# Full-row score products, grouped SSM output products, and new planner prices in a two-block fp32 kernel

## The chip, the cores and the metric

The kernel runs on one core of a Trainium2 chip. The metric is the time of one execution on the device, in microseconds (us). The engines are TensorE (PE: matmuls and transposes; PEld: its weight loads), VectorE (DVE), ScalarE (ACT), GpSimd (POOL) and SyncE (SP, which issues DMAs). Each runs its own instructions in order, and they wait for one another through semaphores.

## What is computed

The reference is two transformer blocks, one after the other, on 512 tokens of 1024 channels, in float32. The first has NSA attention (compressed, selected and windowed keys; at this length the last two reach the same 512 keys), MLA attention and an MLP with squared ReLU; its norms are modulated by `c @ w_ada`. The second has a diagonal state-space mixer (SSM) beside an eight-head attention with a relative bias, then a gated FFN.

```python
# block 1
mod = c @ w_ada + b_ada
h = modulate(rmsnorm(x, g_mix), sh_a, sc_a)
z = h @ w_in
s = einsum('bghqd,bgkd->bghqk', qq, k_win) * scale - slopes * dist
...
y = sigmoid(zga) * (o_nsa @ w_o_nsa) + sigmoid(zgb) * (o_mla @ w_o_mla)
x = x + gt_a * (y @ w_out)
x = x + gt_m * (square(relu(h @ w_fc1)) @ w_fc2)
# block 2
_, states = associative_scan(combine, (a, bu), axis=1)
y = einsum('bsgp,ghp->bsgh', states, c_mat).real + d_skip * uf
...
x = x + mixed @ w_out
x = x + (silu(h2 @ w_gate) * (h2 @ w_up)) @ w_down
```

## The kernel before

**Precision.** A float32 product is done in three passes. A value is split into a rounded high part and a low part (`hilo`, names ending in h and l), and `mm` adds h*h, l*h and h*l in PSUM. Weights arrive as `wr`, become `wh` on ScalarE and `wl` on VectorE, or on POOL for some stages. So the dense layers are rows such as `mm<-hh,wh`, `mm<-hl,wh`, `mm<-hh,wl` of 512 columns.

**How work is ordered.** The kernel's functions do not issue instructions. `Rec` hands each to `Plan.record`, which notes what it reads and writes; `Plan.price` (line 121) gives it a time; `Plan.schedule` (line 159) then plays a list schedule: each engine takes, at its planned free time, the ready instruction of the lowest number, within a window of 500, provided its tiles find a place. An instruction with a second engine (`alt`) goes there if the first would end later. `Plan.issue` emits all in that order; its call stands on line 337, so every row of the profile reads L337 and is told apart by its tiles. The planner's prices decide nothing but this order: on the chip an engine runs its instructions in order and each waits for its semaphores.

**Attention.** `Unit` (line 1256) is one head, or one of two halves of an NSA head (16 units in NSA, 8 in MLA, 8 in the second attention). `qk(i)` writes the scores of query block i into a bank `S` of 128 to 512 columns, by the products that `passes(i)` lists; VectorE adds the bias (`sb`, `st`), ScalarE takes the exponential, `sc` scales, `tr` transposes on PE into a bank `T` (`T<-ident,sb`), `ph` and `pl` are made from it, `pv` multiplies by the values into `O`. `pipeline` (line 1321) staggers three units; dense jobs run between.

A query tile `qA` holds the high part on 64 of the rows and the low part on the other 64. `kA` holds the keys' high part on both halves, so the first product, of 128 rows, gives q_hi*k_hi + q_lo*k_hi. The second takes the 64 rows of q_hi with `kL`, the keys' low part. In NSA `kL` has the low part on both halves. In the second attention `k2l` is one tile for two heads, each on its half.

**SSM.** `ssm(hf)` (line 1905) does half of the channels. X products (`T<-U,rec`, 64 columns wide, 64 of them) turn inputs `U`, read back from DRAM (`ud`), into chunk inputs; VectorE rotates them (`sr`, `si`) and does a scan per pair (`tensor_tensor_scan`); the products by the rotation (`ss`, `st`, on VectorE or POOL) give the states; then the Y products: for each of o and e one bank Y, and for each of four k one product of `U` with 128 rows and two of the states with `pcr` and `pci`, of 64 rows each (rows `T<-U,rec 128*128` and `T<-ss,rec 64*128`), after which ScalarE copies Y.

**The start.** For each of eight tiles of 128 channels, VectorE and POOL sum 1024 rows of `w_ada` weighted by `c` into `aacc` and `aacg` (the weights `aw` come by SP's queue), PE adds these over partitions (`S<-ones,aacc`), VectorE makes the scale `ca`, then scales the tile (`xT`) and splits it (`hh` on ScalarE, `hl` on VectorE). `linT4` multiplies each tile with four weight pieces into four banks as it comes.

Of the kernel before, what the change touches and what calls it, by code (L numbers as in the profile page):

```python
# [19 lines left out]
T = 512  # L20
# [17 lines left out]
BGP = 300  # L38
ORDER = {"N": "Q3 Q2 S3 V0 T0 Q1 S2 V123 F T1 Q0 S1 S0 T23",
# [4 lines left out]
class Op:  # L44
    __slots__ = ("eng", "fn", "a", "kw", "prio", "tiles", "cost", "nbytes", "succ", "npred", "ready", "idx", "alt")


class Plan:
    """Records the instructions of the engines, with what they read and write, and issues them in the order of a
    list schedule: each engine takes the instruction of the lowest number of those whose operands are there."""  # L50
# [24 lines left out]
    def record(self, eng, name, fn, a, kw, alt=None):  # L75
# [39 lines left out]
        o.cost = self.price(o, name, out[0], aps)  # L115
        if alt is not None:
            o.eng = alt
            o.alt = (alt, getattr(self.eng[alt], name), self.price(o, name, out[0], aps))
            o.eng = eng

    def price(self, o, name, out, aps):
        """An estimate of the instruction's time, in us."""
        ins = [x for x in aps if x is not out]
        n = max([x.free_size() if callable(x.free_size) else x.free_size for x in aps]) if aps else 1
        ps = any(x.space == PSUM for x in aps)
        if name == "dma_start":
            sz = 4
            for d in out.shape:
                sz *= d
            o.nbytes = sz  # L130
            return 1.0 if o.eng == "POOL" else 0.06
        if o.eng == "PE":
            l, r = o.a[1], o.a[2]
            if name == "transpose":
                return 0.107 * (out.shape[-1] if len(out.shape) == 2 else 128) / 128
            cols = 1
            for d in r.shape[1:]:
                cols *= d
            if r.dtype == F32R:
                return max(cols, 16) / 2400.0  # L140
            return max(cols * 4 / 2400.0, 0.21 if l.shape[-1] > 64 else 0.107)
        if o.eng == "ACT":
            c = n / 1200.0 + (0.052 if ps else 0.093)
            if name == "activation" and (hasattr(o.kw.get("scale"), "tensor") or hasattr(o.kw.get("bias"), "tensor")):
                c += 0.093
            if o.kw.get("accum_out") is not None:
                c += 0.093
            return c
        if o.eng == "DVE":
            if name in ("tensor_scalar", "tensor_copy") and not ps:  # L150
                return 0.069 + n / 1920.0
            if name == "memset":
                return 0.01 + n / 960.0
            return 0.069 + n / 960.0
        if name == "memset":
            return 0.04 + n / 1200.0
        return 0.12 + n / 250.0 if name == "tensor_scalar" else 0.95 if n <= 8 else 0.15 + n / 475.0

    def schedule(self, window):
        """Operations in the order of their planned starts. A place for a tile is given ahead of its turn only if  # L160
        what comes before that turn can still be run, one by one, in the places that are left."""
# [30 lines left out]
        hw = dma = 0.0  # L192

# [11 lines left out]
        def lacking(i):  # L205
            """The tag of which the operation can't have a place now."""
# [15 lines left out]
        while len(order) < n:  # L222
# [21 lines left out]
            if o.alt is not None and e == o.alt[0]:  # L244
                # the second engine takes it if the first one would end later
# [4 lines left out]
                cost, fn = o.alt[2], o.alt[1]  # L250
            g = lacking(i)
# [17 lines left out]
            end = s + cost  # L269
            free[e] = end  # L270
            if o.nbytes:
# [6 lines left out]
                dma = d + o.nbytes / 360e3  # L278
# [61 lines left out]
class Rec:  # L340
    """An engine whose instructions are recorded; alt is a second engine that may take them."""
# [9 lines left out]
class Later:  # L351
    """Instructions that are to come some steps later in their engine's order."""
# [21 lines left out]
class Weights:  # L374
# [24 lines left out]
    def split_next(self, limit):  # L399
        """Split the next piece into its two parts, if the slots are free."""  # L400
# [36 lines left out]
def merge(gens):  # L437
    """Emit several streams side by side; gens is a list of (generator, total cost)."""
# [18 lines left out]
def offset(plan, g, d):  # L457
    """The stream with its numbers shifted by d."""
# [23 lines left out]
def tile_kernel(ctx: ExitStack, tc: tile.TileContext, A, out):  # L482
# [29 lines left out]
    def early(name):  # L512
        """A tile that may be written long before its turn: these share a few places of their own."""
# [19 lines left out]
    def prio(d):  # L533
        """Instructions that are to come as if traced d instructions later."""
# [5 lines left out]
    # ---------------------------------------------------------------- constants  # L540
# [50 lines left out]
    def rstd_of(acc, n, tag="T"):  # L591
        """[tokens] rsqrt of the mean of squares, along the partitions: [128, 4]."""
# [8 lines left out]
    def spread(r, tag="T"):  # L601
        """[128 tokens, 4] -> the same row of 512 tokens on each partition (in PSUM)."""
# [11 lines left out]
    # ---------------------------------------------------------------- dense jobs  # L614
# [7 lines left out]
    def linT(srcs, kk, nk, xs, evac, mt=2, tag="mm", first=None):  # L622
        """out^T tiles: srcs are pieces [128, kk*(mt*128)]; xs() gives the (hi, lo) list."""
# [21 lines left out]
    def linT4(srcs, kk, nk, xs, evacs, tags=("mm", "mm", "O", "S"), pre=None, vec=None):  # L645
        """Two jobs side by side, k outermost: for inputs that come one after the other."""
# [27 lines left out]
    def linV(srcs, kk, nk, xs, evac, n=256, tag="mm"):  # L674
        """out tiles [128 tokens, n]: x as the stationary operand."""
# [29 lines left out]
    def run(upto):  # L705
        """Emit the jobs up to (not including) number upto."""
# [50 lines left out]
    # ---------------------------------------------------------------- block 1, inputs of the attentions  # L757
# [88 lines left out]
    def q_parts(p, e, scale):  # L846
        """[hi; lo] (or [lo; hi]) of one head of the pair of heads in p; hi stays on its partitions."""
# [83 lines left out]
    # MLA projections  # L931
# [61 lines left out]
    # outputs of the attentions  # L993
# [50 lines left out]
    # MLP  # L1044
# [43 lines left out]
    # block 2  # L1088
# [16 lines left out]
    def qk2_evac(j):  # L1105
        def ev(m, p):
# [118 lines left out]
    def last_gen():  # L1225
        """The last rows of w_down: tokens on the partitions, so that they can leave tile by tile."""
# [125 lines left out]
    def o_fin(key, h, store, cb):  # L1352
        """o of head h = upper + lower half; both heads of a pair go into one tile."""
# [16 lines left out]
    # ---------------------------------------------------------------- start  # L1370
# [12 lines left out]
    def ada0_vec(j):  # L1383
        """Shift and scale of the channels 128 j ..: the products, summed over the tiles of rows."""
# [66 lines left out]
    def go(gen, every=5.0):  # L1451
        """Emit a stream; every so often a step of the background."""
# [19 lines left out]
    # ---------------------------------------------------------------- NSA  # L1472
# [54 lines left out]
    def nsa_units():  # L1527
# [11 lines left out]
        for h in range(8):  # L1539
            g = h // 4  # L1540
            r = 64 * (h % 2)
            for b in range(2):
                def passes(i, b=b, g=g, h=h, r=r):
# [4 lines left out]
                    return [(qA[:, cs], kA[:, :n]), (qA[r:r + 64, cs], kL[r:r + 64, :n])]  # L1548
# [641 lines left out]
```

## Time and profile before

| what | value |
|---|---|
| time, median of 3 runs | 1551.39 us (1551.03 to 1553.93) |
| span of the profiled execution | 1547.8 us |
| mean granted TensorE clock in it | 0.970 of full speed |
| PE busy | 1473.4 us, 95%, 7008 instructions |
| PEld busy | 1193.4 us, 77% |
| DVE busy | 994.4 us, 64%, 1972 instructions |
| ACT busy | 627.0 us, 41% |
| POOL busy | 273.6 us, 18%, 262 instructions |

Busy shares are averages over stages that differ. In time they are: the start (0 to 67 us), projections and the compression MLP (to 138), NSA (to 340), MLA and its outputs (to 468), the MLP (to 940), the SSM's first half (to 997), the second attention with the SSM's second half (to 1116), the mixer's output (to 1180), the FFN (to 1548). A PE row shows a modelled end, and rows overlap; how far apart starts are tells what a product takes.

### The profile page before, as it was taken

The numbers are of one execution on the slowest core, as the hardware profiler recorded it, in microseconds if no ns is written. First come the engines' busy times: TensorE is split into PE (matmuls) and PEld (weight loads), VectorE is DVE, ScalarE is ACT, GpSimd is POOL, SyncE is SP. The second block draws the span as 40 slices with busy tenths as digits, with TensorE's granted clock in tenths as the row PEclk, the third lists the DMA queues.
The fourth block names the chain that finished last, engine by engine and source line by source line (L and its number), as shares of the span: only waits on it lengthen the run. The fifth ranks groups of instructions, "written<-read, shape, count | busy, mean of one in ns | idle before, by whom it ended". The sixth has DMA issues, their size and how long they took to land.

```text
span 1547.8 us, 19040 instructions
## 1 busy us (share of the span) xinstructions
PE 1473.4 (95%) x7008; PEld 1193.4 (77%) x7008; DVE 994.4 (64%) x1972; ACT 627.0 (41%) x1057; POOL 273.6 (18%) x262
## 2 busy tenths in 40 slices
PE   4889999998899999999999998999899999999997
PEld 3687777786688888887787887877688888888885
DVE  7835687877997788766443556296876544553544
ACT  3425556665654342332323431274733322231222
POOL 7514040535200000000213111037031000000000
PEclk9998999999999999999999998699899999999998
DMA  9355252434026422333444665113122333333311
GB/s 368 110 181 173 68 168 84 137 109 170 28 94 202 128 76 89 109 105 126 132 146 160 218 225 109 41 56 116 51 93 82 97 108 90 101 95 110 104 60 55
DMA packets 72604, 184.75 MB, mean 119 GB/s; under 512 B 16792, under 2 KB 17640, under 8 KB 72512
## 3 DMA queue, kind: packets, MB, share of 16 engines
q1 hardware_dynamic: 63424, 158.62, 32.2%
q0 software_dynamic: 7552, 22.97, 4.4%
q10 hardware_dynamic: 1536, 1.95, 0.4%
q8 instruction: 55, 0.90, 0.2%
q14 instruction: 37, 0.30, 0.1%
HBM read 165.41 MB, written 19.67 MB: 120 GB/s over the span
## 4 chain that ended last, share of the span: by engine, by line
PE 78%; DVE 9%; issue 5%; DMA 4%; POOL 2%; ACT 2%; SPq 0%; DVEq 0%; POOLq 0%; ACTq 0%
PE mm L337 64%; PE T L337 7%; PE S L337 4%; PE O L337 3%; DVE sb L337 2%; DMA aw<-in_w_ada 2%; POOL aacg L337 1%; DMA adaw<-in_w_ada 1%; DVE wl L337 1%; DVE pl L337 1%; DVE zqd L337 1%; DMA U<-ud 1%; DVE q L337 1%; DVE sr L337 1%; DVE xt L337 0%
## 5 line engine op out<-in xcount | busy, mean ns | idle before, releaser
L337 PE MATMUL mm<-hh,wh 128*128 128x512 f32 x880 | 363.4, 415 | 13.3 <-ACT hh L337 5.8
L337 ACT CAST wh<-wr 128x1024 fp32r<-128x1024 f32 x209 | 219.2, 1051 | 366.1 <-PE mm L337 331.0
L337 PE MATMUL mm<-hl,wh 128*128 128x512 f32 x880 | 355.1, 403 | 0.2 <-DVE hl L337 0.2
L337 PE MATMUL mm<-hh,wl 128*128 128x512 f32 x880 | 352.8, 401 | 0.5 <-DVE wl L337 0.5
L337 DVE TENSOR_TENSOR wl<-wr,wh 128x1024 fp32r<-128x1024 f32 x199 | 256.3, 1289 | 144.8 <-ACT wh L337 142.3
L337 PEld LDWEIGHTS mm<-hh,wh 128*128 128x128 f32 x880 | 167.9, 192 | 52.6 <-ACT hh L337 6.6
L337 PEld LDWEIGHTS mm<-hh,wl 128*128 128x128 f32 x880 | 168.8, 192 | 37.7 <-issue 1.4
L337 PEld LDWEIGHTS mm<-hl,wh 128*128 128x128 f32 x880 | 169.2, 192 | 34.7 <-issue 2.4
L337 PE MATMUL mm<-fh,wl 128*128 128x512 f32 x416 | 162.5, 391 | 0.0
L337 PE MATMUL mm<-fl,wh 128*128 128x512 f32 x416 | 162.3, 390 | 0.0
L337 PE MATMUL mm<-fh,wh 128*128 128x512 f32 x416 | 161.7, 390 | 0.0
L337 PEld LDWEIGHTS mm<-fh,wh 128*128 128x128 f32 x416 | 78.1, 188 | 16.8 <-issue 0.6
L337 PEld LDWEIGHTS mm<-fh,wl 128*128 128x128 f32 x416 | 78.1, 188 | 16.8 <-issue 0.6
L337 PEld LDWEIGHTS mm<-fl,wh 128*128 128x128 f32 x416 | 78.1, 188 | 16.6 <-DVE PBr L337 0.2
L337 ACT ACTIVATE sb<-sb,st 128x256 f32<-128x256 f32 (+3 forms) x128 | 71.5, 560 | 47.4 <-DVE st L337 46.5
L337 POOL TENSOR_TENSOR adacc<-adacc,adaw 128x1024 f32<-128x1024 f32 x28 | 68.9, 2460 | 55.1 <-ACT adaw L337 54.6
L337 PE MATMUL T<-ident,sb 128*128 128x128 f32 x320 | 57.7, 280 | 11.1 <-DVE sb L337 6.0
L337 DVE TENSOR_TENSOR pl<-T,ph 128x384 fp32r<-128x384 f32 (+1 forms) x96 | 56.9, 595 | 16.5 <-ACT ph L337 13.6
L337 ACT CAST ph<-T 128x384 fp32r<-128x384 f32 (+1 forms) x96 | 49.0, 511 | 44.9 <-PE T L337 35.6
L337 POOL TENSOR_TENSOR st<-st,mhalf 128x1 f32<-128x1 f32 x4 | 2.2, 547 | 358.2 <-DVE st L337 358.2
L337 PEld LDWEIGHTS T<-ident,sb 128*128 128x128 f32 x320 | 40.3, 143 | 22.8 <-DVE pl L337 6.2
L337 DVE CUSTOM_DVE_ANT_0 sb<-S,nb 128x256 f32<-128x256 f32 (+2 forms) x96 | 45.3, 482 | 15.6 <-PE S L337 15.0
(373 smaller groups left out, 2560.4 us busy)
## 6 DMA issues: line engine op xcount, KB each, us to landing
wr<-in_w_fc SPq DMA_DIRECT2D x64, 512.0 KB, 3.6
wr<-in_w_in SPq DMA_DIRECT2D x48, 512.0 KB, 4.4
wr<-in_w_gu SPq DMA_DIRECT2D x44, 512.0 KB, 3.6
adaw<-in_w_ada POOLq DMA_DIRECT2D x32, 512.0 KB, 4.3
wr<-in_w_down SPq DMA_DIRECT2D x22, 512.0 KB, 3.5
aw<-in_w_ada SPq DMA_DIRECT2D x32, 256.0 KB, 6.0
wr<-in_w_out SPq DMA_DIRECT2D x16, 512.0 KB, 3.8
rec<-srec SPq DMA_DIRECT2D x28, 256.0 KB, 5.8
```

The source lines that it names most:

```text
L337: fn(*o.a, **o.kw)
```

## The change

Three things are changed; docstrings and comments go as well, which moves the issuing call from line 337 to 359.

First, the second score product takes all 128 rows, in NSA and in the second attention. It then adds q_lo*k_lo in NSA. In the second attention there is a `k2l` tile for each head, whose other half POOL sets to zero: eight memsets of 64x512 more.

Second, the Y products of the SSM: both banks of an o are open, the eight `U` products stand first, then for each k the four 64-row products of both e.

Third, the planner: other prices; a charge `SWITCH` of 0.2 us when a PE instruction has another count of rows or columns (32, 64 or 128) than the one before it; and a lock `port` between VectorE and POOL, held by VectorE's instructions with two inputs in SBUF, or one in a copy or tensor_scalar, and by all of POOL's but memsets and DMAs.

```diff
+SWITCH = 0.2
...
-            return 1.0 if o.eng == "POOL" else 0.06
+            return 0.6 if o.eng == "POOL" else 0.06
         if o.eng == "PE":
             l, r = o.a[1], o.a[2]
+            m, cut = free(l), lambda v: 32 if v <= 32 else 64 if v <= 64 else 128
+            o.mode = (cut(l.ap[0][1]), 128 if name == "transpose" or r.dtype == F32R else cut(m))
...
-                return max(cols, 16) / 2400.0
+                return max(0.11, free(r) / 2400.0 + 0.0136)
...
+            o.port = len(big) > 1 or (two and len(big) == 1)
...
+        o.port = True
+        if name == "tensor_copy":
+            return 0.06 + n / 1040.0
+        return 0.1 + n / 355.0 if name == "tensor_scalar" else 0.95 if n <= 8 else 0.15 + n / 475.0
...
+            if o.port and port[other[e]] > s:
+                heapq.heappush(f, (port[other[e]], r, i))
+                continue
...
             end = s + cost
+            if e == "PE":
+                end += SWITCH * (o.mode != mode)
+                mode = o.mode
+            if o.port:
+                port[e] = end
...
-                kl = slot(F32R, "k2l")
                 for e in range(2):
-                    kA = slot(F32R, "k2A")
+                    kA, kl = slot(F32R, "k2A"), slot(F32R, "k2l")
                     r, o = e * 64, (1 - e) * 64
+                    gp.memset(f(kl)[o:o + 64], 0.0)
...
-                    return [(qA[:, cs], kA[:, :n]), (qA[r:r + 64, cs], kL[r:r + 64, :n])]
+                    return [(qA[:, cs], kA[:, :n]), (qA[:, cs], kL[:, :n])]
...
+            Y = [bank("T")[:, 0:256].rearrange("p (g c) -> p g c", g=4) for e in range(2)]
             for e in range(2):
...
+                    mm(Y[e][:, k], rec[2 * o + g // 4][:, 128 * (g % 4):128 * (g % 4) + 128], U[:, 8 * o + g], k == 0,
+                       False)
+                yield 0.9
+            for k in range(4):
+                for w, (pc, s_) in enumerate(((pcr, sr), (pci, si))):
+                    for e in range(2):
+                        r = slice(64 * e, 64 * e + 64)
+                        mm(Y[e][:, k], pc[r, 128 * k:128 * k + 128], s_[r, k], False, w == 1)
```

The rows below are the instructions in the order in which they are issued; the number behind a name tells tiles of one name apart.

On PE, at the Y products of the SSM's first half (`rec` 1859 and 1860 are the full-row matrices, 1867 and 1869 are `pcr` and `pci`), before:

```order
L337 MATMUL mm_1896<-hh_1796,wl_1876 128x512
L337 MATMUL T_1898<-ss_1883,rec_1867 128x64
L337 MATMUL mm_1896<-hh_1804,wh_1886 128x512
L337 MATMUL T_1898<-ss_1883,rec_1869 128x64
L337 MATMUL T_1898<-U_1873,rec_1859 128x64
L337 MATMUL T_1898<-ss_1883,rec_1867 128x64
L337 MATMUL T_1898<-ss_1883,rec_1869 128x64
L337 MATMUL T_1898<-U_1873,rec_1860 128x64
```

and with the change:

```order
L359 MATMUL T_1899<-U_1873,rec_1859 128x64 x2
L359 MATMUL T_1899<-U_1873,rec_1860 128x64 x2
L359 MATMUL mm_1896<-hh_1788,wh_1875 128x512
L359 MATMUL mm_1896<-hl_1789,wh_1875 128x512
L359 MATMUL mm_1896<-hh_1788,wl_1876 128x512
L359 MATMUL T_1898<-ss_1883,rec_1867 128x64
L359 MATMUL T_1899<-ss_1883,rec_1867 128x64
L359 MATMUL T_1898<-ss_1883,rec_1869 128x64
L359 MATMUL T_1899<-ss_1883,rec_1869 128x64
```

The `U` products now stand together ahead of the first `ss`, and the 64-row products come by fours of both banks.

On POOL, at the same place, where VectorE does its scans, before:

```order
L337 MEMSET ss_1992 128x512
L337 TENSOR_TENSOR wl_1900<-wr_1851,wh_1899 128x1024
L337 TENSOR_TENSOR wl_1910<-wr_1854,wh_1909 128x1024
L337 TENSOR_TENSOR ss_1894<-sr_1892,rec_1872 128x4x63
L337 TENSOR_TENSOR st_1893<-sr_1892,rec_1872 128x4x63
```

and with the change:

```order
L359 TENSOR_TENSOR ss_1883<-sr_1881,rec_1871 128x4x63
L359 TENSOR_TENSOR st_1882<-sr_1881,rec_1871 128x4x63 x2
L359 TENSOR_TENSOR wl_1910<-wr_1854,wh_1909 128x1024
L359 MEMSET ss_2064 128x512
```

One of the two `wl` has left POOL, and the other stands behind products for the first `ss`.

On VectorE at the start, where the second tile is scaled (`S_182` carries its sums), before:

```order
L337 TENSOR_SCALAR aacc_207<-aw_142,vec 128x256
L337 SCALAR_TENSOR_TENSOR aacc_192<-aw_140,vec,aacc_192 128x256
L337 SCALAR_TENSOR_TENSOR aacc_207<-aw_142,vec,aacc_207 128x256
L337 SCALAR_TENSOR_TENSOR ca<-S_182,ca,vec 128x1
L337 SCALAR_TENSOR_TENSOR aacc_207<-aw_143,vec,aacc_207 128x256
L337 SCALAR_TENSOR_TENSOR xT_117<-xT_117,ca,R_162 128x512
```

and with the change:

```order
L359 SCALAR_TENSOR_TENSOR aacc_217<-aw_189,vec,aacc_217 128x256
L359 SCALAR_TENSOR_TENSOR aacc_225<-aw_199,vec,aacc_225 128x256
L359 SCALAR_TENSOR_TENSOR aacc_225<-aw_200,vec,aacc_225 128x256 x2
L359 SCALAR_TENSOR_TENSOR aacc_225<-aw_201,vec,aacc_225 128x256
L359 SCALAR_TENSOR_TENSOR ca<-S_182,ca,vec 128x1
L359 SCALAR_TENSOR_TENSOR xT_117<-xT_117,ca,R_162 128x512
L359 SCALAR_TENSOR_TENSOR hl_186<-xT_117,mod,hh_185 128x512
```

The sums of all later tiles (`aacc_225` is the last tile's) stand ahead of the second tile's scale.

In counts: five `wl` and three additions of the rotary part move from POOL to VectorE, two `st` the other way; PE's instructions stay the same in number.

More of the change, by code (lines that the diff above doesn't have):

```diff
@@ L44 @@
 class Op:
-    __slots__ = ("eng", "fn", "a", "kw", "prio", "tiles", "cost", "nbytes", "succ", "npred", "ready", "idx", "alt")
+    __slots__ = ("eng", "fn", "a", "kw", "prio", "tiles", "cost", "nbytes", "succ", "npred", "ready", "idx", "alt", "port",
+                 "mode")
 class Plan:
@@ L114, in record @@
         o.npred = len(preds)
-        o.cost = self.price(o, name, out[0], aps)
         if alt is not None:
@@ L119, in record @@
             o.eng = eng
+        o.cost = self.price(o, name, out[0], aps)
     def price(self, o, name, out, aps):
-        ins = [x for x in aps if x is not out]
-        n = max([x.free_size() if callable(x.free_size) else x.free_size for x in aps]) if aps else 1
+        free = lambda x: x.free_size() if callable(x.free_size) else x.free_size
+        n = max([free(x) for x in aps]) if aps else 1
         ps = any(x.space == PSUM for x in aps)
+        o.port, o.mode = False, None
         if name == "dma_start":
@@ L130, in price @@
             o.nbytes = sz
-            return 1.0 if o.eng == "POOL" else 0.06
+            return 0.6 if o.eng == "POOL" else 0.06
         if o.eng == "PE":
             l, r = o.a[1], o.a[2]
+            m, cut = free(l), lambda v: 32 if v <= 32 else 64 if v <= 64 else 128
+            o.mode = (cut(l.ap[0][1]), 128 if name == "transpose" or r.dtype == F32R else cut(m))
             if name == "transpose":
[L135 to L138, printed above, removed]
+                return 0.108
             if r.dtype == F32R:
-                return max(cols, 16) / 2400.0
-            return max(cols * 4 / 2400.0, 0.21 if l.shape[-1] > 64 else 0.107)
+                return max(0.11, free(r) / 2400.0 + 0.0136)
+            return 2 * max(0.111 if m > 64 else 0.055, free(r) / 1200.0 + 0.005)
         if o.eng == "ACT":
@@ L148, in price @@
             return c
+        ins = [x for x in aps if x is not out and x is not o.kw.get("accum_out")]
+        big = [x for x in ins if free(x) > 8 and x.space != PSUM]
+        two = name in ("tensor_scalar", "tensor_copy") and not ps
         if o.eng == "DVE":
-            if name in ("tensor_scalar", "tensor_copy") and not ps:
-                return 0.069 + n / 1920.0
             if name == "memset":
                 return 0.01 + n / 960.0
-            return 0.069 + n / 960.0
+            o.port = len(big) > 1 or (two and len(big) == 1)
+            c = 0.069
+            if name in ("tensor_scalar", "scalar_tensor_tensor"):
+                c += 0.06 * sum(free(x) == 1 for x in ins)
+            return c + n / (1920.0 if two else 960.0)
         if name == "memset":
             return 0.04 + n / 1200.0
-        return 0.12 + n / 250.0 if name == "tensor_scalar" else 0.95 if n <= 8 else 0.15 + n / 475.0
+        o.port = True
+        if name == "tensor_copy":
+            return 0.06 + n / 1040.0
+        return 0.1 + n / 355.0 if name == "tensor_scalar" else 0.95 if n <= 8 else 0.15 + n / 475.0
     def schedule(self, window):
@@ L192, in schedule @@
         hw = dma = 0.0
+        port = {"DVE": 0.0, "POOL": 0.0}
+        other = {"DVE": "POOL", "POOL": "DVE"}
+        mode = (128, 128)
         def offer(i):
@@ L277, in schedule @@
                     d = max(hw + 0.65, dma)
-                dma = d + o.nbytes / 360e3
+                dma = d + o.nbytes / 375e3
                 end = dma + 0.9
@@ L1963, in ssm @@
             sr, si = st[o]
+            Y = [bank("T")[:, 0:256].rearrange("p (g c) -> p g c", g=4) for e in range(2)]
             for e in range(2):
-                Y = bank("T")[:, 0:256].rearrange("p (g c) -> p g c", g=4)
-                r = slice(64 * e, 64 * e + 64)
                 for k in range(4):
                     g = 2 * k + e
-                    mm(Y[:, k], rec[2 * o + g // 4][:, 128 * (g % 4):128 * (g % 4) + 128], U[:, 8 * o + g], True, False)
-                    mm(Y[:, k], pcr[r, 128 * k:128 * k + 128], sr[r, k], False, False)
-                    mm(Y[:, k], pci[r, 128 * k:128 * k + 128], si[r, k], False, True)
-                    yield 0.65
-                act.copy(ye[:, 8 * o + e:8 * o + 8:2], Y)
+                    mm(Y[e][:, k], rec[2 * o + g // 4][:, 128 * (g % 4):128 * (g % 4) + 128], U[:, 8 * o + g], k == 0,
[6 more added lines that the diff above has]
+                        mm(Y[e][:, k], pc[r, 128 * k:128 * k + 128], s_[r, k], False, w == 1)
+                yield 0.9
+            for e in range(2):
+                act.copy(ye[:, 8 * o + e:8 * o + 8:2], Y[e])
         yield 1.0
```

2 lines of the change are left out of this document (1 added, 1 removed).

## The prediction

> **What bounds the kernel now.** I read the page first: the share of each engine, the clock in slices, the chain that ended last. Then the stretches by stage, then single rows.
>
> ```profile
> span 1547.8 us, 19040 instructions
> ...
> PE   4889999998899999999999998999899999999997
> ...
> PEclk9998999999999999999999998699899999999998
> ...
> PE 78%; DVE 9%; issue 5%; DMA 4%; POOL 2%; ACT 2%; SPq 0%; DVEq 0%; POOLq 0%; ACTq 0%
> ```
>
> TensorE is nearly full in every slice and holds 78% of the chain that ended last. So time is won only where TensorE's own work gets shorter, where it stands still, or where its clock is low: the clock is below 0.8 in one slice alone, the 26th (967 to 1006 us).
>
> ```profile
> 138.00:340.00 202.00, 198.83 (x979) 150.80 (x978) 152.89 (x368) 117.76 (x251) 59.82 (x49) 0.98 0.35 114
> 340.00:440.00 100.00, 85.70 (x393) 67.12 (x394) 86.38 (x164) 60.02 (x120) 40.93 (x25) 0.93 0.29 95
> 960.00:997.00 37.00, 37.00 (x119) 30.76 (x120) 7.83 (x19) 3.66 (x7) 2.04 (x3) 0.50 0.02 4
> 997.00:1050.00 53.00, 51.54 (x337) 41.31 (x335) 48.50 (x133) 34.07 (x72) 15.34 (x19) 1.00 0.25 72
> 1050.00:1110.00 60.00, 55.66 (x287) 43.77 (x285) 41.09 (x106) 37.82 (x80) 24.33 (x17) 0.97 0.32 102
> ```
>
> Columns: stretch, length, busy time of PE, PEld, DVE, ACT, POOL, granted clock, DMA share, GB/s. The first stretch is the NSA attention, the second the MLA attention, the third the first half of the SSM, the last two the second attention with the second half of the SSM. In the NSA attention PE has 3.2 us without work, VectorE 49.1: PE is the bound there, VectorE (76%) is next. The third stretch is a surprise: PE is busy for all of it, at half clock, and no other engine has much to do.
>
> **Term A, the score products of the NSA attention.** The second product of a score uses 64 rows; the ones around it use 128.
>
> ```profile
> 204.64 0.39 PE L337 MATMUL mm<-hh,wl 128*128 128x512 f32 x1
> 204.87 0.40 PE L337 MATMUL S<-kA,qA 128*128 128x512 f32 x1
> 205.19 0.50 PE L337 MATMUL S<-kL,qA 64*128 64x512 f32 x1
> 205.62 0.50 PE L337 MATMUL mm<-hh,wh 128*128 128x512 f32 x1
> 205.96 0.40 PE L337 MATMUL mm<-hl,wh 128*128 128x512 f32 x1
> ```
>
> Matmuls overlap, so I take start to start. Two full products of 512 columns are 0.23 apart (204.64 to 204.87). From kA to kL it is 0.32, from kL to the next 0.43, from that to the one after 0.34: 0.09 + 0.20 + 0.11 = 0.40 us more than three full ones would take. That the extra goes with full rows is seen at kA itself: same columns, 128 rows, and among full products it costs the 0.23. There are 16 units of four such products (512, 384, 256 and 128 columns).
>
> ```profile
> L337 PE MATMUL S<-kL,qA 64*128 64x512 f32 x16 | 8.2, 515 | 0.0
> L337 PE MATMUL S<-kL,qA 64*128 64x128 f32 x16 | 5.3, 333 | 0.0
> ```
>
> The 64 of them at 0.40 are 25.6 us on an engine that has no idle time: the upper end, 24 after those whose neighbours have 64 rows already. The new form adds no columns and no instruction. The lower end: PE goes from 199 to about 177 us of work, so VectorE's 153 us come from 76% to 86%, and waits for softmax rows begin to show; in the MLA stretch, where VectorE has 86 of 100 us, PE stands idle 14%. Were half of the gain lost in that way, 12 would be left. I take **-18** (range -24 to -10), since the new order keeps as many PE rows between a unit's scores and its transposes as the old one: the work of some forty wide products, at 0.23 some ten microseconds (an estimate).
>
> **Term B, the SSM's first half.** This is the largest term and the least certain.
>
> ```profile
> 950.70 5.93 DVE L337 TENSOR_TENSOR_SCAN sr<-rho,sr 128x64 f32<-128x64 f32 x8
> ...
> 960.52 1.55 DVE L337 TENSOR_TENSOR_SCAN sr<-rho,sr 128x64 f32<-128x64 f32 x8
> ```
>
> ```profile
> 950.44 4.95 POOL L337 TENSOR_TENSOR wl<-wr,wh 128x1024 fp32r<-128x1024 f32 x2 [23.07 <-PE mm L337]
> ```
>
> ```profile
> 946.69 3.29 PE L337 MATMUL T<-U,rec 128*64 128x64 f32 x64 [3.20 <-DMA U<-ud]
> 949.91 0.39 PE L337 MATMUL mm<-wl,hh 128*128 128x256 f32 x1
> ...
> 958.65 0.43 PE L337 MATMUL T<-ss,rec 64*128 64x64 f32 x2 [3.94 <-DVE ss L337]
> ...
> 960.54 1.11 PE L337 MATMUL T<-ss,rec 64*128 64x64 f32 x4
> 961.58 0.69 PE L337 MATMUL T<-U,rec 128*128 128x64 f32 x2
> 962.20 1.11 PE L337 MATMUL T<-ss,rec 64*128 64x64 f32 x4
> ```
>
> Eight scans took 5.93 us where the next eight, of one shape with them, took 1.55. During the first eight POOL held two `wl` subtractions, 950.44 to 955.39. So the scans lost 4.4 us to POOL, and PE stood idle 3.94 us until the first `ss`. Right behind that idle time the clock falls:
>
> ```profile
> 955.00:960.00 5.00, 1.35 (x6) 0.92 (x6) 5.00 (x18) 0.00 (x0) 0.39 (x1) 0.96 0.50 165
> 960.00:965.00 5.00, 5.00 (x19) 4.29 (x19) 4.54 (x15) 0.00 (x0) 2.04 (x3) 0.50 0.01 3
> ...
> 990.00:995.00 5.00, 5.00 (x15) 3.99 (x15) 0.00 (x0) 0.72 (x2) 0.00 (x0) 0.50 0.15 26
> 995.00:1000.00 5.00, 5.00 (x19) 4.01 (x18) 2.15 (x3) 2.02 (x3) 0.00 (x0) 0.78 0.35 101
> ```
>
> It stays at 0.50 for about 37 us, though PE is busy by the page all that time. In the new order POOL takes three `ss`/`st` products in place of the `wl` next to them, one `wl` goes to VectorE, and 24 products of 256 columns and 9 of 512 stand between the X products and the first `ss`; the scans then run free. If the 4.4 us go, the 3.94 us go with them, and there is no idle time that could drop the clock.
>
> What then remains from 949.91 to 997.3? 4.8 us ran at full clock before the idle time, 0.9 just after it, and 37 us at half clock hold 18.5 us of work: 24.2 in place of 47.4, a gain of 23.2. The grouped Y products change the row count less often: 7 blocks of `ss` in place of some 30 pairs, each pair now with 64-row neighbours for four at 0.26 us (1.04 / 4, half clock). At full clock that saves 1 to 2 us more. If the clock falls all the same, the stretch keeps its half clock and gains 3.9 (idle time) plus 2 to 4 (grouping at half clock), some -7; with a stall left over, -4. I take **-21** (range -25 to -4): the row nearest to the new mixture is the second half of the SSM, where groups of `ss`, U and three wide products ran in the stretch 997 to 1050 at clock 1.00.
>
> The Trainium skill, "TensorE: Matmul & The Clock Gate", Part 1, says that the clock rises again after one busy window of about 3.4 us. By that rule the half clock would have ended near 963 and B would be worth an estimated 7 us; the windows from 960 to 995, busy 5.00 of 5.00 at 0.50, do not agree with it for this mixture of small products, so I go by the windows.
>
> **Term C, the second attention and the SSM's second half.**
>
> ```profile
> L337 PE MATMUL S<-k2l,qA 64*128 64x512 f32 x8 | 4.0, 496 | 0.0
> ```
>
> The 32 `k2l` score products (8 units of four widths) lose the same up to 0.40 each, 12.8 us at most; several stand side by side already, so 9 to 11. Grouping the 32 Y pairs gives another 1 to 3. But VectorE has 48.5 of 53 us in the first of these stretches, against PE's 51.5. So VectorE takes over after some 3 us there; in the second one it has 41.1 of 60 and gains hold, up to the data that the tail after 1100 waits for. I take **-6** (range -14 to -2).
>
> ```profile
> 55.74 0.52 POOL L337 MEMSET VC<- 128x512 f32 x1
> ```
>
> The eight new memsets of half a `k2l` are put on POOL, which is busy 15.3 of 53 us: hidden beside PE. No row has a memset of 64x512; the nearest, of 128x512, took 0.52 us, so 8 x 0.5 = 4 us of POOL, nothing of PE (at worst one late `k2l`, 0.5 us). [...]
>
> **Term D, the start.** Here the new order speaks against the change.
>
> ```profile
> 22.80 0.22 DVE L337 SCALAR_TENSOR_TENSOR ca<-S,ca,vec 128x1 f32<-128x1 f32 x1 [0.68 <-ACT mod L337]
> ...
> 29.62 0.22 DVE L337 SCALAR_TENSOR_TENSOR ca<-S,ca,vec 128x1 f32<-128x1 f32 x1
> ...
> 47.66 2.43 DVE L337 SCALAR_TENSOR_TENSOR aacc<-aw,vec,aacc 128x256 f32<-128x256 f32 x3
> 50.02 0.20 DVE L337 SCALAR_TENSOR_TENSOR ca<-S,ca,vec 128x1 f32<-128x1 f32 x1
> ...
> 64.32 0.75 DVE L337 SCALAR_TENSOR_TENSOR hl<-xT,mod,hh 128x512 fp32r<-128x512 f32 x1 [1.00 <-ACT hh L337]
> ```
>
> Before, the second `ca` came at 29.62 and the fifth at 50.02, with the weighted sums `aacc` between. Now all sums, the last of which ended at 50.09 before, stand ahead of the second `ca`. Taking out three `ca`, three scalings and three `hl` (3 x (0.2 + 0.75 + 0.75) = 5 us) puts that second `ca` at about 45, and until then PE has only the first tile's products.
>
> ```profile
> L337 DVE TENSOR_TENSOR wl<-wr,wh 128x1024 fp32r<-128x1024 f32 x199 | 256.3, 1289 | 144.8 <-ACT wh L337 142.3
> ```
>
> From there each of seven tiles takes 2.7 us on VectorE (0.2 + 0.75 + 1.00 of waiting for ScalarE's `hh` + 0.75), less where the wait is filled, and two `wl` of 1.29 stand among them: the last `hl` at 64 to 68, against 65.07 now. PE's 12 products for a tile take 12 x 0.23 = 2.8 us, so it keeps up, at half clock for the first of them. **+2**, range -2 to +8.
>
> **Term E, the rest of the reordering.** In MLA three scalings on VectorE took 3.06 us each beside POOL's work, where one of that shape (`hl` at 64.32) took 0.75:
>
> ```profile
> 342.84 9.17 DVE L337 SCALAR_TENSOR_TENSOR zqd<-zqd,vec,R 128x512 f32<-128x512 f32 x3 [0.39 <-ACT R L337]
> ```
>
> ```profile
> 354.05 0.50 PE L337 MATMUL mm<-hh,wh 128*128 128x512 f32 x1 [2.55 <-ACT tg L337]
> ```
>
> PE stood idle for 2.55 us just when they ended, for a ScalarE result. A `wl` leaves POOL there. -2, range -6 to +6, for stalls of this size that go or come.
>
> **The sum.** -18 - 21 - 6 + 2 - 2 = -45, from the span of 1547.8 to 1502.8. The median of the runs, 1551.39, lies 3.6 above the span; the same 3.6 added gives **1506.4**.
>
> **The rivals.**
> 1. *The half clock comes back* in the SSM's first half: another idle time of about 3 us before the first `ss`, or the 3.2 us wait for U ahead of it. B is -7: the time is 1520. For it: the mixture never raised the clock by itself. Against it: the wait for U, 3.2 us, left the clock high before. 18%.
> 2. *VectorE becomes the bound* in both attentions: A -10, C -2, E +2, B -21: 1551.4 - 29 = 1522. For it: 92% in the stretch from 997. Against it: 76% in the longer one. 17%.
> 3. *The order gives all back*: the planner's new prices move work between units, and PE waits at the end of a unit as it does in MLA (2.55 us before 354.05). There are 24 units with changed scores. It decides from 45 / 24 = 1.9 us a unit; at 2.55 us each, 61 us are lost and the time is 1567, slower than before. For it: MLA's 14% idle. Against it: the ten microseconds of cover in the order. 7%.
> 4. *The change does nothing to the row switches*, say because a full-row product costs what the 64-row one did: A and C 0, B -7, and the new order wavers about 0: 1544 to 1552. Against it: kA at 0.23. 4%.
>
> The forecast itself has 54%; its own range is 1492 to 1518, from the ends of the terms that vary most (B by 4, A by 6, C by 4, D and E by 6). The range for 8 in 10 takes in rivals 1 and 2 and the lower ends: **1487 to 1533**. A measurement of this kernel tells 0.2% (3 us) from no change. Faster by more: 89%; within: 4%; slower: 7%.
>
> **What would show it.** A: rows of `S<-kL` read 128 rows and start 0.23 from their neighbours, and the NSA stretch is 16 to 22 us shorter. B: eight scans of about 1.6 us, no wait of some 4 us for `ss`, and a slice clock of 0.9 where 0.6 stood. C: the stretch from the Y products to the glu 4 to 10 us shorter. D: the second `ca` near 45. I am wrong if the clock is 0.5 behind the X products, if waits for VectorE fill the NSA stretch, or if the start ends beyond 75.

## The result and the profile after

The changed kernel takes 1506.28 us (median of 4 runs, 1503.7 to 1514.51) against 1551.21 us; the ratio is 0.972, with a 95% interval of 0.969 to 0.976. The profiled execution has a span of 1512.7 us and is the slowest of the four. A second profile of the same kernel, taken with the experiments, has 1505.6 us; where the two differ, both are shown.

From the page of the changed kernel, the span, PE and its clock in 40 slices, and the chain that ended last:

```profile
span 1512.7 us, 19050 instructions
...
PE   3798999997899999999999998989999999999996
...
PEclk9999899999999999999999999699899999999998
...
PE 76%; DVE 8%; ACT 4%; issue 3%; DMA 2%; POOL 1%; SPq 0%; DVEq 0%; POOLq 0%; ACTq 0%
```

PE is as full as before; it simply has less to do. To see where the time went, I cut each trace at the same five rows: the first and the last `S<-kA` (NSA), the first `mm<-fh,wh` (the MLP's second layer), the end of the first 64 X products of the SSM, the first `S<-k2A` (second attention) and the first `mm<-mxh,wh` (the mixer's output). Lengths in us, from the rows' starts:

| stretch | before | change | change, second profile | term, forecast |
|---|---|---|---|---|
| start to NSA | 138.3 | 145.6 | 146.4 | D, +2 |
| NSA scores | 188.6 | 170.3 | 168.2 | A, -18 |
| to the MLP | 259.8 | 257.9 | 260.4 | E, -2 |
| to the X products' end | 363.3 | 360.9 | 363.0 | |
| SSM, first half | 51.4 | 38.2 | 26.7 | B, -21 |
| second attention, SSM's second half | 122.2 | 116.2 | 117.4 | C, -6 |
| the rest | 424.3 | 423.5 | 423.5 | |

The timeline of PE in the changed kernel, at a pair of scores:

```profile
200.12 0.49 PE L359 MATMUL S<-kA,qA 128*128 128x512 f32 x1
200.44 0.40 PE L359 MATMUL S<-kL,qA 128*128 128x512 f32 x1
200.67 0.34 PE L359 MATMUL S<-kA,qA 128*128 128x384 f32 x1
200.85 0.34 PE L359 MATMUL S<-kL,qA 128*128 128x384 f32 x1
```

From `kL` to the next product are 0.23 us now, at 384 columns 0.18; the 0.43 of before is gone. (The 0.32 ahead of it belongs to `kA`, whose neighbour was a product of one column.)

VectorE and POOL at the SSM's scans, same kernel:

```profile
935.90 1.56 DVE L359 TENSOR_TENSOR_SCAN sr<-rho,sr 128x64 f32<-128x64 f32 x8
...
939.91 2.58 DVE L359 TENSOR_TENSOR ss<-sr,rec 128x252 f32<-128x252 f32 x1
```

```profile
939.67 2.54 POOL L359 TENSOR_TENSOR wl<-wr,wh 128x1024 fp32r<-128x1024 f32 x1
```

The scans are free (1.56 us for eight). But the `wl` that is left on POOL now meets one `ss`, which takes 2.58 us in place of 0.41. PE waits 1.47 us for it:

```profile
941.34 0.40 PE L359 MATMUL mm<-hh,wl 128*128 128x512 f32 x1
943.20 0.66 PE L359 MATMUL T<-ss,rec 64*128 64x64 f32 x8 [1.47 <-DVE ss L359]
```

The windows behind that wait (length, busy PE, PEld, DVE, ACT, POOL, clock, DMA share, GB/s), first profile of the change:

```profile
940.00:945.00 5.00, 3.53 (x25) 2.32 (x23) 5.00 (x13) 0.00 (x0) 2.74 (x2) 0.93 0.33 92
945.00:950.00 5.00, 5.00 (x29) 4.00 (x29) 3.12 (x7) 0.37 (x2) 0.00 (x0) 0.50 0.22 43
...
960.00:965.00 5.00, 5.00 (x23) 3.41 (x22) 0.00 (x0) 0.65 (x2) 0.00 (x0) 0.50 0.00 0
965.00:970.00 5.00, 5.00 (x16) 3.91 (x16) 1.23 (x1) 1.05 (x1) 0.00 (x0) 0.68 0.15 26
```

and of the second, where the same wait is 0.45 us:

```profile
945.67 0.66 PE L359 MATMUL T<-ss,rec 64*128 64x64 f32 x8 [0.45 <-DVE ss L359]
```

```profile
945.00:950.00 5.00, 4.55 (x40) 3.29 (x40) 5.00 (x18) 0.18 (x1) 0.47 (x2) 1.00 0.36 108
950.00:955.00 5.00, 5.00 (x42) 4.29 (x41) 1.27 (x2) 0.84 (x3) 0.00 (x0) 1.00 0.31 105
```

In one execution the half clock came back, for some 24 us; in the other it did not. That is 11.5 us between the two columns of the table, about as much as the four runs lie apart (10.8).

Both executions have the same order, and in both VectorE loses some 2.2 us beside that `wl`. In the first the `wl` starts 0.24 us ahead of the `ss`, which takes 2.58 us; in the second it starts 0.08 us behind it, and the two additions that follow take 2.92 us in place of 0.74:

```profile
942.44 2.57 POOL L359 TENSOR_TENSOR wl<-wr,wh 128x1024 fp32r<-128x1024 f32 x1 [0.28 <-ACT wh L359]
```

```profile
942.36 0.41 DVE L359 TENSOR_TENSOR ss<-sr,rec 128x252 f32<-128x252 f32 x1
942.69 2.92 DVE L359 TENSOR_TENSOR ss<-ss,st 128x252 f32<-128x252 f32 x2
```

What differs is when PE gets there. Its 64 X products, first profile and second:

```profile
932.71 2.08 PE L359 MATMUL T<-U,rec 128*64 128x64 f32 x64 [2.91 <-DMA U<-ud]
```

```profile
934.69 3.31 PE L359 MATMUL T<-U,rec 128*64 128x64 f32 x64 [3.79 <-DMA U<-ud]
```

and the clock over them, first profile and second:

```profile
930.00:935.00 5.00, 2.29 (x66) 2.25 (x67) 1.59 (x5) 0.36 (x1) 0.00 (x0) 1.00 1.26 192
```

```profile
935.00:940.00 5.00, 5.00 (x76) 4.88 (x73) 3.67 (x15) 0.13 (x1) 0.15 (x1) 0.66 1.10 90
```

In the second the wait for U was longer, the clock fell there already, and the X products took 1.2 us more. From their start PE needed 9.0 us to come to the `ss` in the first execution and 10.5 in the second, and VectorE had the `ss` ready after 10.5 and 11.0 us. So the shorter wait comes from a slower PE ahead of it, not from a faster VectorE.

The start, VectorE's `ca` rows of the changed kernel:

```profile
41.63 0.21 DVE L359 SCALAR_TENSOR_TENSOR ca<-S,ca,vec 128x1 f32<-128x1 f32 x1
...
48.55 0.22 DVE L359 SCALAR_TENSOR_TENSOR ca<-S,ca,vec 128x1 f32<-128x1 f32 x1 [4.10 <-PE S L359]
...
53.20 0.22 DVE L359 SCALAR_TENSOR_TENSOR ca<-S,ca,vec 128x1 f32<-128x1 f32 x1 [1.87 <-PE S L359]
...
59.78 0.22 DVE L359 SCALAR_TENSOR_TENSOR ca<-S,ca,vec 128x1 f32<-128x1 f32 x1 [3.94 <-PE S L359]
```

and PE's rows between the first two of them:

```profile
41.90 0.79 PE L359 MATMUL S<-hh,wh 128*128 128x512 f32 x1 [8.73 <-DVE ca L359]
...
47.56 0.39 PE L359 MATMUL S<-hh,wl 128*128 128x512 f32 x1
47.79 0.28 PE L359 MATMUL S<-ones,aacg 128*128 128x1 f32 x2
```

The second scale comes at 41.6. But the third waits 4.10 us for PE: its sums (`S<-ones`) stand in PE's order behind the products of the tile before. So each tile goes round a loop of PE, VectorE, ScalarE and PE, and the last product of this layer ends at 77.7 (78.6 in the second profile), not at 67.4.

### The profile page after: what moved, and what is told of

Its sections match the earlier page's. It is cut to its first block, busy times and chain, and to the rows that moved or that the text cites. A ratio compares the mean times of both kernels' runs of the same rounds, so it can differ in the third digit from the quotient of the medians.

```text
span 1512.7 us, 19050 instructions
## 1 busy us (share of the span) xinstructions
PE 1426.5 (94%) x7008; PEld 1175.6 (78%) x7008; DVE 985.2 (65%) x1978; ACT 627.9 (42%) x1057; POOL 263.9 (17%) x264
## 4 chain that ended last, share of the span: by engine, by line
PE 76%; DVE 8%; ACT 4%; issue 3%; DMA 2%; POOL 1%; SPq 0%; DVEq 0%; POOLq 0%; ACTq 0%
PE mm L359 65%; PE T L359 5%; PE S L359 3%; PE O L359 3%; DVE sb L359 2%; DMA adaw<-in_w_ada 1%; POOL adacc L359 1%; DVE pl L359 1%; DVE wl L359 1%; ACT sb L359 1%; ACT wh L359 1%; DVE xt L359 0%; DVE q L359 0%; DVE st L359 0%; DVE sr L359 0%
## 5 line engine op out<-in xcount | busy, mean ns | idle before, releaser
L359 PE MATMUL mm<-hh,wh 128*128 128x512 f32 x880 | 359.0, 409 | 7.5 <-ACT hh L359 3.3
L359 DVE TENSOR_TENSOR wl<-wr,wh 128x1024 fp32r<-128x1024 f32 x204 | 265.7, 1305 | 124.9 <-ACT wh L359 123.0
L359 ACT ACTIVATE sb<-sb,st 128x128 f32<-128x128 f32 (+3 forms) x128 | 71.8, 562 | 43.8 <-DVE st L359 43.0
L359 PEld LDWEIGHTS T<-ident,sb 128*128 128x128 f32 x320 | 39.8, 143 | 22.4 <-issue 7.5
L359 DVE TENSOR_TENSOR swg<-mm,R 128x512 f32<-128x512 f32 x21 | 14.5, 692 | 61.1 <-PE mm L359 61.1
```

Of the source, the lines that this page charges most:

```text
L359: fn(*o.a, **o.kw)
```

## The experiments

### The three parts, each alone

Is the gain that of full rows and grouping, or of the planner's order? Each part was put alone into the kernel before, and the changed kernel was run again beside them.

The scores alone:

```diff
-                    return [(qA[:, cs], kA[:, :n]), (qA[r:r + 64, cs], kL[r:r + 64, :n])]
+                    return [(qA[:, cs], kA[:, :n]), (qA[:, cs], kL[:, :n])]
...
+                    kA, kl = slot(F32R, "k2A"), slot(F32R, "k2l")
+                    gp.memset(f(kl)[o:o + 64], 0.0)
```

> The kernel before with only the full-row score products (and the eight memsets that they need). Theory 1 (each row change on PE costs 0.1 to 0.2 us of an engine without idle time): the NSA stretch, first to last score product, is 18 to 24 us shorter, the second attention 4 to 8; the start (last linT4 product at 67) and the 37 us of half clock in the SSM's first half stay. Time about 1526. Theory 2 (VectorE is the bound of the attentions, and the gain in NSA of the change came from its new order): NSA at most 8 us shorter, time about 1540.

1525.87 us, ratio 0.985 (0.983 to 0.987).

The grouped Y products alone:

```diff
-                    mm(Y[:, k], rec[2 * o + g // 4][:, 128 * (g % 4):128 * (g % 4) + 128], U[:, 8 * o + g], True, False)
-                    mm(Y[:, k], pcr[r, 128 * k:128 * k + 128], sr[r, k], False, False)
-                    mm(Y[:, k], pci[r, 128 * k:128 * k + 128], si[r, k], False, True)
+            for k in range(4):
+                for w, (pc, s_) in enumerate(((pcr, sr), (pci, si))):
+                    for e in range(2):
+                        mm(Y[e][:, k], pc[r, 128 * k:128 * k + 128], s_[r, k], False, w == 1)
```

> The kernel before with only the grouped Y products of the SSM. Theory 1 (the two subtractions on POOL still hold up the scans, PE still idles 4 us, the clock still falls to half, grouping only saves row changes): 4 to 8 us in both halves together, time about 1545, half clock still some 30 us behind the idle time. Theory 2 (grouping in itself keeps the clock up or ends the half clock early): the half clock lasts under 15 us, time about 1533.

1533.37 us, ratio 0.989 (0.986 to 0.993).

The planner alone (prices, charge and lock of the change, with products as before):

```diff
+SWITCH = 0.2
...
+            if o.port and port[other[e]] > s:
+                heapq.heappush(f, (port[other[e]], r, i))
+                continue
...
+                end += SWITCH * (o.mode != mode)
```

> The kernel before with only the planner's new prices, row-change charge and lock; the 64-row score products and the Y products one by one stay. Theory 1 (the planner loses some 10 us at the start, by sums ahead of the second tile's scale, and wins some at the SSM's scans): last linT4 product at 76 to 78, scans of 1.6 us, time between 1538 and 1552. Theory 2 (most of the gain is the planner's order, which puts fewer row changes next to each other): time about 1530.

1566.74 us, ratio 1.012 (1.008 to 1.015): slower than before, by more than theory 1 allowed.

> The changed kernel, unedited, for a second profile beside the first, whose execution was the slowest of four (span 1512.7, times 1503.7 to 1514.5). Theory 1 (the start's loss of 10 us and the half clock of about 23 us in the SSM's first half are parts of this kernel): both are there again, and the spread of some 10 us lies in stretches at half clock that differ between executions. Theory 2 (they are accidents of that one execution): the last linT4 product is near 68 or the half clock is gone, and the span is about 1500.

1507.36 us, ratio 0.974 (0.971 to 0.977). So theory 1 holds for the start and theory 2 for the half clock.

Differences to the kernel before, in us, by the same rows as above:

| stretch | scores | grouping | planner | sum of the three | change, second profile |
|---|---|---|---|---|---|
| start to NSA | +0.6 | -0.2 | +9.1 | +9.5 | +8.1 |
| NSA scores | -17.0 | +0.1 | +4.1 | -12.8 | -20.4 |
| SSM, first half | +0.4 | -16.1 | -1.9 | -17.6 | -24.7 |
| second attention, SSM's second half | -5.7 | -4.0 | +4.2 | -5.5 | -4.8 |

The scores bring nearly what A and C said: 17.0 in NSA, a little under the 18 of theory 1. PE, VectorE and ScalarE run their instructions in exactly the order of before in this kernel, so this gain owes nothing to the order.

Grouping came out close to its theory 2: about 1533 us and under 15 us of half clock were expected, 1533.37 us and 16 us were measured, though PE still idles 2.82 us behind scans of 5.90 us. The profiled execution is the fastest of its four, 6.8 us below their median, so the 16.1 us of the table is the upper end.

The planner by itself loses in the start and in both attentions. Against the sum of the three, the change's second profile is 7.6 us shorter in NSA and 7.1 in the SSM; its first is 5.5 shorter in NSA and 4.4 longer in the SSM. So the three don't simply add up. By the medians of these runs the scores win 23.4 us, grouping wins 15.9 and the planner loses 17.4, which makes 21.9, and the whole change wins 41.9. That full rows and grouping would win their 39.3 us with the planner of before too is likely but not shown: the kernel with both and without the planner's part was not run.

### The start, and what holds the clock

The start's loss was laid to the lock: the planner holds it for whole instructions, and so plans POOL's sums late. In `late_lock` it is on only behind the first layer:

```diff
+        self.lock = False
...
+        o.port = o.port and self.lock
...
     go(run(1))
+    plan.lock = True
     go(run(5))
```

> The changed kernel with the planner's VectorE/POOL lock switched on only behind the first layer's start, so that the sums of the start are planned as before (the other new prices stay). Theory 1 (the lock, which the planner holds for whole instructions, plans POOL's sums too late and so puts the second tile's scale behind all of VectorE's sums): last linT4 product back at 67 to 70, the second scale near 30, time about 1498. Theory 2 (other prices, of pointer scalars or of PE's small products, do it): last linT4 product still at 76 to 79, time about 1506.

1492.68 us, ratio 0.962 (0.960 to 0.965), and the four runs lie within 1.2 us (1491.92 to 1493.12). VectorE's scales in its timeline:

```profile
26.12 0.22 DVE L361 SCALAR_TENSOR_TENSOR ca<-S,ca,vec 128x1 f32<-128x1 f32 x1 [0.27 <-ACT mod L361]
33.43 0.22 DVE L361 SCALAR_TENSOR_TENSOR ca<-S,ca,vec 128x1 f32<-128x1 f32 x1 [0.27 <-PE S L361]
38.88 0.20 DVE L361 SCALAR_TENSOR_TENSOR ca<-S,ca,vec 128x1 f32<-128x1 f32 x1
```

The second scale comes at 26.12 in place of 41.63, and no scale waits more than 0.7 us. The layer's last product ends at 63.8: 14.8 us earlier than in the change's second profile, and 3.6 earlier than before the change. The stretch to NSA is 133.3 us long. That is theory 1, and more than it expected.

Next, the last `wl` of 2.5 us was taken off POOL beside the SSM:

```diff
-    W.on_gp = True
     go(run(j_v2))
     go(merge([(ssm(0), 36.0), (run(j_att2), 20.8)]))
+    W.on_gp = True
```

> The kernel of late_lock, with the weights' low parts of the stage around the SSM's first half made on VectorE alone, so that no subtraction of 1024 columns stands on POOL beside the products for ss. Theory 1 (the remaining idle time ahead of the first ss, 0.5 to 1.5 us, comes from that subtraction, and the half clock of up to 24 us follows idle time ahead of small products): the first ss starts without a wait over 0.5 us, no half clock behind it, first ss to last ss about 12 us as in the better profile of the change, time 1494 to 1498 with little spread. Theory 2 (the half clock is set by the wait for U ahead of the X products, which stays): it comes in some executions as before, time as late_lock.

1492.48 us, ratio 0.963 (0.960 to 0.965). PE has no idle time ahead of the first `ss` and there is no half clock behind it. But late_lock, with a wait of 0.72 us, had no half clock either, so the times are the same and the run decides between neither theory.

Then the lock and the charge were taken away one by one, in the changed kernel:

```diff
-            if o.port and port[other[e]] > s:
+            if False and port[other[e]] > s:
```

> The changed kernel with no lock between VectorE and POOL in the planner, all else kept. Theory 1 (the lock costs the start 9 us, and elsewhere its gain is small, since the full rows and the grouping carry the change): last linT4 product at 67 to 70, time 1497 to 1502. Theory 2 (the lock is what keeps POOL's long subtractions from the scans): scans near 4 to 6 us again, idle time of 3 us or more ahead of ss, half clock over 30 us, time 1510 or more.

1501.19 us, ratio 0.968 (0.966 to 0.970). Scans of 1.56 us without the lock as well: theory 2 falls. The start wins its time back (64.0), but the NSA stretch is 175.3 us long, 7.1 more than with the lock. So the lock is worth 7 us in NSA and costs the stretch up to NSA 11.8 (134.6 against 146.4). That it does so by planning POOL's sums late is argued from its code; the runs show only that the lock does it.

```diff
-SWITCH = 0.2
+SWITCH = 0.0
```

> The changed kernel with the planner's charge for a change of rows or columns set to 0, all else kept. Theory 1 (few changes are left once scores take full rows and Y products are grouped, so the charge decides little): time within 4 us of the change. Theory 2 (the charge keeps the rest of the 64-row and small products together): the Y products scatter again among wide products, SSM stretches 5 us longer or more, time 1512 or more.

1510.71 us, ratio 0.974 (0.970 to 0.977), against 0.974 for the change: no difference that can be told. The Y products did not scatter: the SSM's first half takes 26.7 us, as in the change's second profile. That is theory 1.

### Idle time or alternating products?

One question was open: does the half clock in the SSM follow from idle time, as the forecast had it, or from the products themselves? The kernel with no stall at all got the Y products one by one again.

```diff
-            Y = [bank("T")[:, 0:256].rearrange("p (g c) -> p g c", g=4) for e in range(2)]
+                Y = bank("T")[:, 0:256].rearrange("p (g c) -> p g c", g=4)
+                    mm(Y[:, k], rec[2 * o + g // 4][:, 128 * (g % 4):128 * (g % 4) + 128], U[:, 8 * o + g], True, False)
+                    mm(Y[:, k], pcr[r, 128 * k:128 * k + 128], sr[r, k], False, False)
+                    mm(Y[:, k], pci[r, 128 * k:128 * k + 128], si[r, k], False, True)
```

> The kernel of late_lock_low_parts_on_vector with the Y products one by one again, as in the kernel before, so that the scans are free and yet U and 64-row products alternate. Theory 1 (the half clock follows idle time ahead of the first ss; without it, full clock): no half clock behind the first ss, first to last ss 15 to 18 us, time 1495 to 1502. Theory 2 (the alternation itself, small products that drain the array again and again, brings or keeps the half clock, and grouping is what cured it): half clock for 15 us or more behind the first ss, first to last ss 25 us or more, time 1505 or more.

1513.26 us, ratio 0.978 (0.977 to 0.980), some 21 us behind the same kernel with grouping; 17.0 of them lie in the SSM's first half (42.9 us in place of 25.9). Its PE rows from the first `ss` on show no wait, and its windows show the clock:

```profile
930.27 0.66 PE L361 MATMUL T<-ss,rec 64*128 64x64 f32 x4
930.85 0.43 PE L361 MATMUL T<-U,rec 128*128 128x64 f32 x2
931.22 0.66 PE L361 MATMUL T<-ss,rec 64*128 64x64 f32 x4
931.80 0.43 PE L361 MATMUL T<-U,rec 128*128 128x64 f32 x2
```

```profile
930.00:935.00 5.00, 4.91 (x30) 4.02 (x29) 5.00 (x17) 0.37 (x1) 1.19 (x2) 1.00 0.01 3
935.00:940.00 5.00, 5.00 (x28) 4.25 (x28) 1.17 (x2) 0.37 (x1) 0.00 (x0) 0.90 0.68 206
940.00:945.00 5.00, 5.00 (x17) 4.14 (x17) 0.00 (x0) 0.00 (x0) 0.00 (x0) 0.50 0.01 3
...
955.00:960.00 5.00, 5.00 (x16) 4.17 (x17) 0.00 (x0) 0.37 (x1) 0.00 (x0) 0.50 0.00 0
```

Some nine microseconds of alternating products bring the clock down, with PE busy for 4.91 us or more of every 5. That is theory 2. The table puts this profile beside the others. Its half clock is twice the lost share of the clock, times the length, between the X products' end and the first `S<-k2A`:

| kernel | Y products | wait ahead of the first ss, us | mean clock, length | half clock, us |
|---|---|---|---|---|
| before | one by one | 3.94 | 0.63, 51.4 | 38 |
| scores_alone | one by one | 4.35 | 0.64, 51.8 | 38 |
| planner_alone | one by one | 2.58 | 0.66, 49.6 | 34 |
| one_by_one_without_stall | one by one | none | 0.72, 42.9 | 24 |
| ygroup_alone | grouped | 2.82 | 0.78, 35.3 | 16 |
| change | grouped | 1.47 | 0.69, 38.2 | 24 |
| change, second profile | grouped | 0.45 | 0.99, 26.7 | under 1 |
| late_lock | grouped | 0.72 | 1.00, 26.7 | none |

One by one, the half clock comes with or without idle time. Grouped, it came only behind waits of 1.47 us and more, and in seven profiles with waits of 0.72 us at most it lasted under 2 us. That the wait causes it there is not shown: the same two profiles also waited least for the X products' input, 2.91 and 2.24 us, where the seven others waited 3.73 to 4.73.

### Two more versions

```diff
     W.on_gp = True
+    plan.lock = False
     go(run(j_pair + 1))
...
     W.on_gp = False
+    plan.lock = True
     go(run(j_out))
```

> The kernel of late_lock with the planner's lock off in the MLA stage as well. Theory 1 (the 4.7 us that the MLA stretch between its first down-projected product and its first output product loses in late_lock, and not in no_lock, are the lock's): that stretch 55 to 56 us again instead of 59.9, time about 1488. Theory 2 (they are the row charge's, since no_row_charge has not got them either): no change there, time 1492 to 1493.

1494.30 us, ratio 0.966 (0.964 to 0.967). The stretch from the first product of the down-projected tiles to the first output product is 56.1 us, as theory 1 says, in place of 59.9; but 2.9 us are lost between the last NSA score product and that first one (45.2 in place of 42.3), and the sum is no better.

> The kernel of late_lock with the charge for a change of rows or columns at 0. Theory 1 (the charge costs MLA 4 us and wins 2 in the second attention): time 1489 to 1492. Theory 2 (the charge decides the small products' order at the start or in the SSM): time over 1496.

1493.49 us, ratio 0.965 (0.963 to 0.967), the runs from 1486.48 to 1495.27. The profiled execution (span 1484.7) wins the 4 us of MLA (56.2), but the median doesn't show them. The best version that can be told apart remains late_lock's order: 57 us below the kernel before in the same runs (1492.68 against 1549.56), some 15 below the change (0.962 against 0.972, of 1550).

## Why the prediction was right, and where its steps were not

The time was forecast at 1506.4 us, and 1506.28 was measured. That close is luck. In the second profile A and B gave 6.1 us more than forecast and D cost 6.1 more, so two errors cancel; in the first B gave 7.8 less, and its span lies 9.9 us above the forecast 1502.8.

- **A, -18: right, mechanism and size.** -18.3 and -20.4 in the two profiles. The scores alone, in the order of before, give -17.0, so it is the rows that pay. The price of 0.40 us was too high for most: PE's work in the stretch, its length less its idle time, fell by 20.1 to 21.5 us in these three profiles, 0.31 to 0.34 for each of 64 products. Idle time ate 1.1 to 3.8 us of it, less than the discount allowed. VectorE, busy 82% of the stretch, did not become the bound: rival 2 falls, though the order is worth a few us there (no_lock is 7.1 us longer).
- **B, -21: the size right on average, the reason half wrong.** -13.2 in the first profile, -24.7 in the second. The stall at the scans went as said, also by POOL's new order. But the forecast read the half clock as the effect of 3.94 us of idle time, and put grouping at 1 to 2 us beside it. The runs show the reverse weight: grouping alone, with the stall left in, is worth up to 16.1 us in this stretch, and taking only the grouping away costs 17.0. "There is no idle time that could drop the clock" is the step that failed: alternating products drop it while PE is busy. And the remaining wait, for an `ss` that meets the other `wl`, was not seen; in one execution of two the half clock came back behind it, which is rival 1 in part. Two readings were wrong besides. The parts of the sum (4.8, 3.9, 0.9 and 37) leave 0.8 of the 47.4 us uncounted, so the gain by that working is 22.4 us and not 23.2. And the wait for U did not leave the clock high before, as rival 1's "against it" has it; the kernel before, over the X products:

```profile
946.00:949.30 3.30, 2.61 (x49) 2.64 (x51) 0.60 (x2) 0.00 (x0) 0.00 (x0) 0.50 1.40 150
```

- **C, -6: right.** -6.0 and -4.8. The scores give -5.7 of it, grouping -4.0, and the planner takes 4.2 when alone.
- **D, +2: wrong.** +10.3 and +11.2 at the layer's last product, +7.4 and +8.1 up to NSA. The second `ca` came at 41.6, where 45 was said. The step that failed is "so it keeps up": PE's products of a tile were counted as 2.8 us beside the next tile's work, but the next tile's sums stand behind them on PE, and so they lie in one chain with `ca`, the scaling and the split. The waits of 4.10, 1.87 and 3.94 us are that chain.
- **E, -2: right within its range.** -1.9 and +0.6 between NSA and the MLP. The stretch up to the X products gave 2.4 and 0.3 that no term had.
- **Rival 3 (the order gives all back)** did not come in this kernel. In the planner alone it did: 1566.74 us, in the start and in both attentions. That the new prices suit full rows better than 64 is the likely reading; no run shows why.

What stays open: whether the wait of 1.47 us itself brought the half clock back in the change's first profile, and which prices make the planner's order better with full rows. The row charge is not it: with the charge at 0 and the lock on, NSA takes 168.2 us in the changed kernel and 167.8 in late_lock, as with the charge. The lock's 7 us are shown, but with the lock on the planner of planner_alone still lost 4.1 us in NSA with 64 rows.

## What to carry to other kernels

Count changes of the matmul's row number on a full PE: here each 64-row product among full ones cost 0.31 to 0.34 us of PE's work in NSA, and in the second attention zeros in the other half were cheaper than a smaller product. Put small products of one row count together, since here their alternation also took the clock. A planner's lock for a shared resource should be tried stage by stage: the same rule won 7 us in one stage and lost 12 in another of one kernel.

## What the runs showed of the hardware

In one_by_one_without_stall PE's clock fell to 0.50 with PE busy for 4.91 to 5.00 us of every 5, behind some nine microseconds of 64-row and 128-row products of 64 columns in turn, and stayed there for 24 us, wide products among them. In the four kernels with the products one by one it came up only 2.8 to 5.0 us behind the last 64-row product of that half. It isn't the width alone: the 64 X products have 64 columns too, but one row count. They start 0.03 us apart at full clock (2.08 us for 64), and in the kernel before the clock came up from 0.50 while they ran (0.50 from 946.0 to 949.4, the products from 946.69 to 949.98). In the alternation four `ss` products take 0.58 us and two of `U` 0.37, that is 0.15 to 0.18 us each. The Trainium skill, "TensorE: Matmul & The Clock Gate", Part 1, ties the clock to how busy PE has recently been. No run shows what is counted as busy; the profile's 5.00 of 5.00 us, with modelled ends, is not it.

Also, VectorE and POOL don't always shut each other out for a whole instruction. Eight scans beside two `wl` lost 4.4 us. But in the start of the changed kernel, from 25 to 40 us, both engines worked at once, at 4.90 to 5.00 of 5.00 us each, and VectorE's sums with two inputs took 0.47 to 0.95 us there, 0.66 on average:

```profile
35.00:40.00 5.00, 0.00 (x0) 0.00 (x0) 5.00 (x9) 0.00 (x0) 5.00 (x7) 1.00 1.05 392
```
